# A streaming encoder step on one core: the bias table written DRAM to DRAM, and 512-column products for v and the FFN's second product

## The chip, the cores and the metric

The kernel runs on one core of a Trainium2 chip. Time is device time in microseconds (us) of one execution, lower is better. The core has TensorE (PE in the profile, with PEld for its weight loads), VectorE (DVE), ScalarE (ACT), GpSimd (POOL) and SyncE (SP). The engines run their own instruction streams in order and meet at semaphores. SP and ACT also issue DMA transfers (SPq, ACTq in the profile); the transfers themselves run on 16 DMA engines.

## What is computed

One layer of a streaming encoder for 640 tokens: 512 of a prompt and 8 samples of 16 each, with the same weights. The reference, cut to what the change touches:

```python
def rel_bias_lookup(table, rel):
    idx = jnp.clip(rel, -A_MAX_REL, A_MAX_REL) + A_MAX_REL      # 257 distances for each of 8 heads
    return jnp.transpose(table[idx], (2, 0, 1)).astype(jnp.float32)
...
    h = rmsnorm(x, lw['norm_mix'])
    a_qkv, b_qkv, b_beta, b_dec, b_gate, c_z, c_xbc, c_dt, gates = split_cols(h @ lw['w_in'], IN_SPLITS)
    aq, ak, av = [t.reshape(bsz, L, A_HEADS, A_HEAD_DIM) for t in jnp.split(a_qkv, 3, axis=-1)]
    ya = band_attn_prompt(aq, ak, av, lw['a_rel_bias'])         # s = q k * scale + bias; softmax; p v
...
    x = x + m @ lw['w_out']
    x = x + memory_attn(rmsnorm(x, lw['norm_x']), mem_k, mem_v, lw['wx_q'], lw['wx_o'])
    hf = rmsnorm(x, lw['norm_ffn'])
    u, gf = jnp.split(hf @ lw['w_up'], 2, axis=-1)
    gf, f_conv_new = causal_dwconv(gf, f_conv, lw['f_conv_w'], lw['f_conv_b'])
    x = x + (u * jax.nn.silu(gf)) @ lw['w_down']
```

The layer has three branches (chunk attention, a gated delta rule, a state-space scan), a merge, cross attention, an FFN of width 2816, and a final norm. All data are float32.

## The kernel before

Each large matrix product is made of three products in a reduced type, fp32r: both factors are split into a high part (`wh`, `hh`, `xTh`) and a low part (`wl`, `hl`, `xTl`), and high by high, low by high and high by low are accumulated in PSUM. ACT makes the high part of a weight piece (`split_w`, a copy), DVE or POOL the low part (a subtraction). A weight piece is loaded by SP into one of two `raw` buffers; the parts go to pool `wp`, six buffers for each, or to a pool of general buffers where `loose` is set. A raw buffer is free again when POOL has made the last low part from it.

There are two forms of product. `fmj` has the weight as stationary operand and streams the 640 tokens in two pieces of 320 columns. `tmj` has a tile of 128 tokens as stationary operand and streams 256 columns of weight: this is used for v (`attn_v`, PSUM name `tm`), for the output projections (`add_proj`, name `ap`) and for the FFN's second product (`add_proj` and `last_proj`, name `dn`). `add_proj` takes the 1024 output columns in four quarters; in a quarter the five token tiles go by pairs, and DVE adds each result to `x`. In the FFN the inner width comes in blocks of 8, 8 and 6 pieces of 128. `last_proj` does the last block and the final norm: after the first 512 columns ACT sums squares (`sumsq`), POOL multiplies `x` by the gain, and then the other 512 columns go pair by pair, each pair followed by its norm on DVE (`inv_rms`) and its store.

The bias table: `rel_table` loads 8 rows of 257 to 8 partitions, pads them to 384 columns on DVE, and ACT issues one store (`relt<-rel`) that writes every row 128 times to DRAM. `prompt_bias` and `attn_sample` read diagonals from it (`rel_ap`), so that each partition has its row shifted by one.

The order around the change is set in `run`: v's weights (columns 1024 to 1535 of `w_in`) are loaded and split between the norms of the token tiles; then v; then `attn_dense` for four head pairs (PSUM name `aps`, q and then k, each with one raw load; the copy out of PSUM is `aqk` on ACT, and k is transposed on PE as `t5a`); `decays` (name `dps`) is between the first and the second pair. Most of the further program is emitted by generators that are pumped beside each other, and a scheduler sets the final order of each engine.

Of the kernel before, what the change touches and what calls it, by code (L numbers as in the profile page):

```python
# [23 lines left out]
NFF = 22  # L24
EPS = 1e-6
NEG = -3.0e38
FA, FS, FB, FC, FP, FX = 0.3, 0.85, 0.95, 1.8, 1.2, 0.5
NGA, NGB, NGC = 5, 3, 5
FN, FR = 3, 1.8
FBS, FCP, FCS = 1.4, 0.9, 1.5  # L30
NWS = 1
LS, LC, LX = 3, 3, 3
SEQ = (0, 1, 2, 4, 3)
LQ = 1
SKA = 1
MAGIC = float(0x5F3759DF)

# [6 lines left out]
class Enc:  # L44
# [41 lines left out]
    def add(self, name, gen, after=()):  # L86
        self.units.append((name, gen, set(after)))
# [116 lines left out]
    def load2(self, out, in_):  # L204

# [216 lines left out]
    def rel_table(self):  # L422


        self.relt = self.dr.tile([P, 8, 384], F32, name="relt")
        t = self.U("rel", shape=(8, 384))
        self.load(t[:, 127:384], self.I["a_rel_rev"])
        self.nc.vector.tensor_copy(t[:, 0:127], t[:, 127:128].broadcast_to([8, 127]))
        self.store(self.relt.rearrange("q h c -> h q c"), t.unsqueeze(1).broadcast_to([8, P, 384]))

    def rel_ap(self, h, nq, c0, n):

        return bass.AP(tensor=self.relt.tensor, offset=self.relt.offset + h * 384 + 127 + c0,
                       ap=[[8 * 384 - 1, nq], [1, n]])
# [945 lines left out]
    def attn_sample(self):  # L1380
        nc, I = self.nc, self.I
        V4, qbd, ksm = self.V[4], self.qbd, self.ksm
        bc = self.U("bsc", shape=(P, 512))
        b16 = self.SM("b16", [P, 16])
        for hh in range(8):
            self.load(bc[16 * hh:16 * hh + 16, 384:], self.rel_ap(hh, 16, 0, P))
            self.load(b16[16 * hh:16 * hh + 16, :], self.rel_ap(hh, 16, P, 16))
        nc.gpsimd.tensor_copy(bc[:, 0:384], bc[:, 384:385].broadcast_to([P, 384]))

        bn = [self.U("bsn", shape=(P, 4, P)) for _ in range(2)]  # L1390
        for b in range(8):
# [82 lines left out]
            yield from self.weave(*([scores(b + 1)] if b < 7 else []), out(b), lead=LS if b < 7 else 0)  # L1474


    def add_proj(self, w, X, x, k0=0, nk=NK, nm="ap", tiles=range(NT), t0=0, engs=None, cols=range(4), last=None,
                 late=False):

        for c in cols:  # L1480
            def cb(pair, ps):
                for j, t in enumerate(pair):
                    xv = x[t][c // 2][:, (c % 2) * 256:(c % 2) * 256 + 256]
                    self.tt(xv, xv, ps[:, j, :256], ALU.add)
            wk = self.weights(w, c * 256, 256, k0, nk, engs)
            yield from self.tmj(lambda: wk, X, cb, tiles=tiles, nm=nm, t0=t0, late=late and c == cols[0])
# [200 lines left out]
    def ffn(self, x, X):  # L1687
        I, O = self.I, self.O
        wu, wd = I["w_up"][0], I["w_down"][0]
        lt = None  # L1690
        for f0, n in ((0, 8), (8, 8), (16, 6)):
            H = []
            for f in range(f0, f0 + n):
# [3 lines left out]
                s = []  # L1697
# [17 lines left out]
                yield from self.fmj(lambda: self.weights(wu, FF + f * P, P, 0, NK), X, gate, nm="fps", split=first)  # L1715
                yield from self.fmj(lambda: self.weights(wu, f * P, P, 0, NK), X, up, nm="ups", split=first)
            if f0 + n < NFF:
                yield from self.add_proj(wd, H, x, k0=f0, nk=n, nm="dn", late=True)
            else:
                yield from self.last_proj(wd, H, x, f0, n)  # L1720

    def last_proj(self, w, H, x, k0, nk):

        nc, O = self.nc, self.O
        g = self.grow(self.I["norm_final"])
        ss = self.SM("fss", [P, 3, NT])
        yield from self.add_proj(w, H, x, k0=k0, nk=nk, nm="dn", cols=(0, 1), late=True)
        for t in range(NT):
            self.sumsq(x[t][0], ss[:, 0, t:t + 1])
            self.tt(x[t][0], x[t][0], g[0], ALU.mult, nc.gpsimd)  # L1730
        wks = [self.weights(w, c * 256, 256, k0, nk, loose=c == 3) for c in (2, 3)]
        for pair in ((0, 1), (2, 3), (4,)):
            for c in range(2):
                def cb(pair, ps):
                    for j, t in enumerate(pair):
                        xv = x[t][1][:, c * 256:(c + 1) * 256]
                        self.tt(xv, xv, ps[:, j, :256], ALU.add)
                        self.sumsq(xv, ss[:, 1 + c, t:t + 1])
                yield from self.tmj(lambda: wks[c], H, cb, tiles=pair, nm="dn")
            r = self.inv_rms(ss[:, :, pair[0]:pair[-1] + 1])  # L1740
            for i, t in enumerate(pair):
                dst = O["y_prompt"][0, t * P:(t + 1) * P] if t < 4 else O["y_sample"].rearrange("b s d -> (b s) d")
                self.stt(x[t][1], x[t][1], r[:, i:i + 1], g[1], ALU.mult, ALU.mult)
                self.act(x[t][0], x[t][0], scale=r[:, i:i + 1])
                for j in range(2):
                    self.load(dst[:, j * 512:(j + 1) * 512], x[t][j])


    def run(self):
        I = self.I  # L1750
        all_ = lambda gen: [None for _ in gen]
# [195 lines left out]
```

## Time and the profile before

| | before |
|---|---|
| time, median of 3 runs | 1810.25 us (1808.98 to 1810.54) |
| time of the profiled execution | 1809.45 us |
| its span | 1807.7 us, 34056 instructions |
| PE busy | 1691.8 us, 94% of the span |
| PEld, DVE, ACT, POOL busy | 88%, 48%, 36%, 34% |
| mean DMA rate | 101 GB/s, 182.41 MB |

The span is what the trace covers; the profiled execution's time has 1.75 us more around it. A busy PE is the union of its matmuls' spans, which overlap, so that the spacing between their starts tells more than the length of one.

### The profile page before, as it was taken

To read this page: it belongs to the slowest core of one execution; us is meant where nothing else is said; L and a number is where in the kernel's file an instruction comes from. 1 tells how busy PE (TensorE), PEld (TensorE's weight loads), DVE (VectorE), ACT (ScalarE), POOL (GpSimd) and SP (SyncE) were. 2 spreads that over 40 slices of the span, in tenths; PEclk is the share of its full clock that TensorE was granted. 3 is DMA by queue.
4 is the path that set the end of the run, shared out by engine and by line. 5 is a ranking of instruction groups with operands and counts; after the bars stand their busy time and mean duration, and the time that the engine had idled before them with its cause. 6 is when DMAs were issued, how large, how long until landed. Compare 5 with 4: busy or idle time off the path is not lost.

```text
span 1807.7 us, 34056 instructions
## 1 busy us (share of the span) xinstructions
PE 1691.8 (94%) x13705; PEld 1585.8 (88%) x13705; DVE 862.5 (48%) x1778; ACT 652.3 (36%) x1611; POOL 613.3 (34%) x644
## 2 busy tenths in 40 slices
PE   6689999999999998999999889999989999999997
PEld 6577778888988888999999889987789999999997
DVE  5025764246777684665444463243574413431443
ACT  4024444422433432343442245332433313331333
POOL 4043322222333353453433235211144334433433
PEclk9889999999999999999999999999999999999999
DMA  5442127422321344235223335246332222212222
GB/s 157 65 113 56 50 84 257 160 67 61 79 80 52 96 123 117 74 110 147 67 74 92 137 120 160 64 170 223 116 106 73 81 71 73 81 60 77 87 78 77
DMA packets 239309, 182.41 MB, mean 101 GB/s; under 512 B 13314, under 2 KB 211983, under 8 KB 239151
## 3 DMA queue, kind: packets, MB, share of 16 engines
q1 hardware_dynamic: 216192, 164.69, 30.1%
q10 hardware_dynamic: 22958, 15.54, 3.3%
q8 instruction: 108, 1.77, 0.4%
q14 instruction: 51, 0.41, 0.1%
HBM read 162.04 MB, written 16.58 MB: 99 GB/s over the span
## 4 chain that ended last, share of the span: by engine, by line
PE 69%; DVE 10%; DMA 3%; ACT 3%; issue 2%; POOL 1%; ACTq 0%; POOLq 0%; SPq 0%; DVEq 0%
PE ups L210 9%; PE fps L210 8%; PE gps L210 8%; PE dn L210 8%; PE pps L210 6%; PE ap L210 5%; PE tm L210 4%; PE qps L210 3%; PE cps L210 2%; DVE xc L221 2%; PE bps L210 2%; PE pl L210 1%; DVE t L218 1%; PE py L210 1%; DMA raw<-in_wx_v_dram 1%
## 5 line engine op out<-in xcount | busy, mean ns | idle before, releaser
L218 POOL TENSOR_TENSOR wl<-raw,wh 128x512 fp32r<-128x512 f32 x376 | 496.5, 1329 | 973.9 <-ACT wh L224 750.5
L224 ACT ACTIVATE wh<-raw 128x512 fp32r<-128x512 f32 x400 | 248.3, 629 | 601.2 <-PE dn L210 94.6
L210 PE MATMUL dn<-wh,hh 128*128 128x256 f32 x440 | 125.1, 284 | 0.4
L210 PE MATMUL dn<-wl,hh 128*128 128x256 f32 x440 | 124.7, 283 | 0.5 <-POOL wl L218 0.5
L210 PE MATMUL dn<-wh,hl 128*128 128x256 f32 x440 | 124.5, 283 | 0.0
L221 DVE SCALAR_TENSOR_TENSOR xc<-xp,vec,xc 128x664 f32<-128x664 f32 (+1 forms) x116 | 117.3, 1011 | 3.2
L210 PE MATMUL gps<-xTh,wh 128*128 128x320 f32 x448 | 117.0, 339 | 0.0
L210 PE MATMUL gps<-xTh,wl 128*128 128x320 f32 x448 | 106.4, 316 | 0.0
L210 PE MATMUL gps<-xTl,wh 128*128 128x320 f32 x448 | 105.3, 314 | 0.0
L541 DVE TENSOR_SCALAR xc<-xp,vec 128x656 f32<-128x656 f32 (+1 forms) x34 | 32.3, 950 | 131.8 <-ACT xp L224 131.8
L210 PEld LDWEIGHTS dn<-wh,hh 128*128 128x128 f32 x440 | 84.4, 192 | 1.3 <-DVE x L218 1.0
L210 PEld LDWEIGHTS dn<-wl,hh 128*128 128x128 f32 x440 | 84.4, 192 | 0.9 <-POOL wl L218 0.9
L210 PEld LDWEIGHTS dn<-wh,hl 128*128 128x128 f32 x440 | 84.4, 192 | 0.0
L210 PEld LDWEIGHTS gps<-xTh,wh 128*128 128x128 f32 x448 | 73.8, 192 | 11.4 <-issue 10.6
L210 PE MATMUL ups<-fTh,wl 128*128 128x320 f32 x352 | 82.0, 310 | 0.0
L210 PE MATMUL fps<-fTh,wh 128*128 128x320 f32 x352 | 82.0, 310 | 0.0
L210 PE MATMUL ups<-fTl,wh 128*128 128x320 f32 x352 | 82.0, 310 | 0.0
L210 PE MATMUL ups<-fTh,wh 128*128 128x320 f32 x352 | 81.7, 310 | 0.0
L210 PE MATMUL fps<-fTh,wl 128*128 128x320 f32 x352 | 81.5, 309 | 0.0
L210 PE MATMUL fps<-fTl,wh 128*128 128x320 f32 x352 | 81.5, 309 | 0.0
L218 DVE TENSOR_TENSOR x<-x,dn 128x256 f32<-128x256 f32 x60 | 23.0, 418 | 118.5 <-PE dn L210 118.5
L210 PEld LDWEIGHTS gps<-xTh,wl 128*128 128x128 f32 x448 | 76.0, 190 | 0.9 <-issue 0.8
(517 smaller groups left out, 4564.0 us busy)
## 6 DMA issues: line engine op xcount, KB each, us to landing
raw<-in_w_in_dram SPq DMA_DIRECT2D x72, 512.0 KB
raw<-in_w_up_dram SPq DMA_DIRECT2D x44, 512.0 KB
raw<-in_w_down_dram SPq DMA_DIRECT2D x20, 512.0 KB
ck<-in_cache_attn_k_dram SPq DMA_DIRECT2D x32, 256.0 KB
cv<-in_cache_attn_v_dram SPq DMA_DIRECT2D x32, 256.0 KB
xck<-in_cache_mem_k_dram SPq DMA_DIRECT2D x32, 256.0 KB
xcv<-in_cache_mem_v_dram SPq DMA_DIRECT2D x32, 256.0 KB
raw<-in_wx_o_dram SPq DMA_DIRECT2D x14, 512.0 KB
```

The costliest lines, as they stand in the source:

```text
L210: self.nc.tensor.matmul(out, lhsT=lhsT, rhs=rhs, start=start, stop=stop)
L218: return (eng or self.nc.vector).tensor_tensor(out, a, b, op=op)
L221: self.nc.vector.scalar_tensor_tensor(out, a, s, b, op0=op0, op1=op1)
L224: self.nc.scalar.activation(out, in_, f, **kw)
L541: nc.vector.tensor_scalar(acc[:, :n], xp[:, :n], taps[0], bias, op0=ALU.mult, op1=ALU.add)
```

## The change

`rel_table` no longer goes through SBUF: one DMA from DRAM to DRAM, on SP's queue, writes the 8 by 257 table 128 times, 8224 bytes at a time and without padding, and a second small one loads the outermost value of each head to all partitions (`far`). The pad is made where it is used: after the load of a diagonal, DVE overwrites the part left of the diagonal by `copy_predicated` with a mask, and POOL fills the far columns from `far` and not from the loaded tile. The sample part gets four small DVE instructions more. `wmj` is new: 512 columns, the inner dimension as outer loop, and all five token tiles accumulated at once in five PSUM banks. `add_proj` uses it where the columns come in halves, which is the FFN's second product; the two other output projections keep quarters. `attn_v` and the second half of `last_proj` use 512 columns with one tile after another. In `last_proj` DVE and POOL share the low parts of the last weights.

```diff
+QUARTERS = ((0, 256), (256, 256), (512, 256), (768, 256))
...
+    def wmj(self, w, c0, X, cb, k0=0, nk=NK, tiles=range(NT), nm="tm", t0=0, engs=None):
+        tiles = list(tiles)
+        acc = []
+        for i in range(0, len(tiles) - 1, 2):
+            ps = self.PD(nm)
+            acc += [(tiles[i], ps[:, 0]), (tiles[i + 1], ps[:, 1])]
+        if len(tiles) % 2:
+            acc.append((tiles[-1], self.PP(nm)))
+        for k in range(nk):
+            if k % 2 == 0:
+                wk = self.weights(w, c0, 512, k0 + k, min(2, nk - k), engs)
+            wh, wl = wk[k % 2]
+            xh, xl = X[k]
+            for t, ps in acc:
+                s = slice((t - t0) * P, (t - t0 + 1) * P)
+                for p, (a, b) in enumerate(((xh, wh), (xl, wh), (xh, wl))):
+                    self.mm(ps, a[:, s], b, start=(k == 0 and p == 0), stop=(k == nk - 1 and p == 2))
+            yield 0.69 * len(acc)
+        self.tick()
+        for t, ps in acc:
+            cb(t, ps)
...
     def rel_table(self):
-        self.relt = self.dr.tile([P, 8, 384], F32, name="relt")
-        t = self.U("rel", shape=(8, 384))
-        self.load(t[:, 127:384], self.I["a_rel_rev"])
-        self.nc.vector.tensor_copy(t[:, 0:127], t[:, 127:128].broadcast_to([8, 127]))
-        self.store(self.relt.rearrange("q h c -> h q c"), t.unsqueeze(1).broadcast_to([8, P, 384]))
+        rev = self.I["a_rel_rev"]
+        self.relt = self.dr.tile([P, 8, A_REL], F32, name="relt")
+        self.load(self.relt.rearrange("q h c -> q (h c)"), rev.rearrange("h c -> (h c)").partition_broadcast(P))
+        self.far = self.C("far", [P, 8])
+        self.load(self.far, rev[:, 0].partition_broadcast(P))
...
@@ prompt_bias
-            nc.gpsimd.tensor_copy(b[:, 0:256], b[:, 256:257].broadcast_to([P, 256]))
+            far = self.far[:, 2 * p + h:2 * p + h + 1]
+            nc.gpsimd.tensor_copy(b[:, 0:256], far.broadcast_to([P, 256]))
+            nc.vector.copy_predicated(b[:, 256:384], self.ms.bitcast(I32), far.broadcast_to([P, P]))
             nc.vector.memset(b[0:64, 448:512], NEG)
...
@@ attn_v
-            for c in range(2):
...
-                yield from self.tmj(lambda: wks[c], X, cb, tiles=pair)
+            ps = self.PD("tm")
+            for j, t in enumerate(pair):
+                for k, (wh, wl) in enumerate(wks):
...
+                        self.mm(ps[:, j], a[:, t * P:(t + 1) * P], b, start=(k == 0 and p == 0),
+                                stop=(k == NK - 1 and p == 2))
...
@@ ffn, last_proj
-                yield from self.add_proj(wd, H, x, k0=f0, nk=n, nm="dn", late=True)
+                yield from self.add_proj(wd, H, x, k0=f0, nk=n, nm="dn")
...
-        wks = [self.weights(w, c * 256, 256, k0, nk, loose=c == 3) for c in (2, 3)]
+        wk = [a for k in range(0, nk, 2) for a in self.weights(w, 512, 512, k0 + k, 2, (nc.vector, nc.gpsimd), loose=k >= 4)]
```

Outside the replaced parts the order of the engines is nearly the same before and after: on PE some thirty rows move by a few places, all of them between v and the sample attention.

The first place is SP's queue at the start, behind the loads of `x`. `raw_258` and `raw_268` are the second half of v's weights, the next two raws those of the first head pair. Before:

```order
L227 DMA x_105<-in_x_sample_dram 128x512
L227 DMA x_107<-in_x_sample_dram 128x512
L227 DMA raw_258<-in_w_in_dram 128x4x256
L227 DMA raw_268<-in_w_in_dram 128x4x256
L227 DMA raw_618<-in_w_in_dram 128x8x128
L227 DMA raw_681<-in_w_in_dram 128x8x128
```

And after:

```order
L252 DMA x_105<-in_x_sample_dram 128x512
L252 DMA x_107<-in_x_sample_dram 128x512
L252 DMA relt<-in_a_rel_rev_dram 128x2056
L252 DMA far<-in_a_rel_rev_dram 128x8x1
L252 DMA raw_258<-in_w_in_dram 128x2x512
L252 DMA raw_268<-in_w_in_dram 128x2x512
```

The table and `far` now stand ahead of the last two weight loads of v.

The second place is ACT from the end of v to the copy of the first pair's k (`aqk_739` before, `aqk_610` after), for which PE's transposes `t5a` wait. Before:

```order
L224 ACTIVATE wh_687<-raw_681 128x512
L230 DMA relt<-rel_608 8x128x384
L224 ACTIVATE V_345<-tm_580 128x256
L224 ACTIVATE aqk_676<-aps_617 128x640
L230 DMA out_dram<-V_345 128x512
L224 ACTIVATE wh_852<-raw_850 128x512
L224 ACTIVATE wh_856<-raw_850 128x512
L224 ACTIVATE wh_954<-raw_952 128x512
L224 ACTIVATE wh_958<-raw_952 128x512
L224 ACTIVATE aqk_739<-aps_680 128x640
```

And after:

```order
L249 ACTIVATE V_345<-tm_452 128x512
L255 DMA out_dram<-V_345 128x512
L249 ACTIVATE wh_725<-raw_723 128x512
L249 ACTIVATE wh_729<-raw_723 128x512
L249 ACTIVATE aqk_547<-aps_488 128x640
L249 ACTIVATE wh_827<-raw_825 128x512
L249 ACTIVATE wh_831<-raw_825 128x512
L249 ACTIVATE wh_889<-raw_887 128x512
L249 ACTIVATE wh_893<-raw_887 128x512
L249 ACTIVATE aqk_610<-aps_551 128x640
```

The store of the table is gone from ACT, and the splits of three raw loads, not of two, stand ahead of the copy for which PE waits.

The third place is the last half of the last FFN block, on POOL and on PE. On POOL `x_` by `grow_` are the gain products of the first 512 columns, `wl_` low parts of the last weights. Before:

```order
L218 TENSOR_TENSOR x_11346<-x_11346,grow_19516 128x512
L218 TENSOR_TENSOR x_11350<-x_11350,grow_19516 128x512
L218 TENSOR_TENSOR wl_19783<-raw_19780,wh_19782 128x512
L218 TENSOR_TENSOR wl_19787<-raw_19780,wh_19786 128x512
L218 TENSOR_TENSOR wl_19793<-raw_19790,wh_19792 128x512
```

And after:

```order
L243 TENSOR_TENSOR x_11228<-x_11228,grow_18890 128x512
L243 TENSOR_TENSOR x_11232<-x_11232,grow_18890 128x512
L243 TENSOR_TENSOR x_11236<-x_11236,grow_18890 128x512
L243 TENSOR_TENSOR wl_19065<-raw_19058,wh_19064 128x512
```

On PE after the change, twelve products into `dn_19068` (the second half's first tile) precede these:

```order
L235 MATMUL dn_19137<-wh_19040,hh_18165 128x512
L235 MATMUL dn_19068<-wh_19060,hh_18738 128x512
L235 MATMUL dn_19068<-wh_19060,hl_18739 128x512
L235 MATMUL dn_19137<-wh_19040,hl_18166 128x512
L235 MATMUL dn_19068<-wl_19061,hh_18738 128x512
L235 MATMUL dn_19068<-wh_19064,hh_18886 128x512
L235 MATMUL dn_19068<-wh_19064,hl_18887 128x512
L235 MATMUL dn_19068<-wl_19065,hh_18886 128x512
```

The low part that POOL makes behind all five gain products, `wl_19065`, is now taken as PE's twentieth product of the half; before, the low parts behind the gain products belonged to the last quarter.

## Rows read from the trace of the kernel before

**Rows 1.** The page, busy time of each engine (share of the span) and instructions.

```profile
PE 1691.8 (94%) x13705; PEld 1585.8 (88%) x13705; DVE 862.5 (48%) x1778; ACT 652.3 (36%) x1611; POOL 613.3 (34%) x644
```

**Rows 2.** Timeline of PE, 57 to 100 us: start, length, instruction [idle before <-releaser].

```profile
57.07 0.46 PE L210 MATMUL aps<-xTh,wh 128*128 128x320 f32 x2
...
71.24 1.26 PE L210 MATMUL dps<-xTh,rawd 128*32 128x320 f32 x10
99.00 1.12 PE L215 MATMUL t5a<-ident,aqk 128*128 128x128 f32 x4 [26.49 <-ACT aqk L224]
```

**Rows 3.** Timeline of ACT, 55 to 100 us.

```profile
55.87 0.54 ACTq L230 DMA_DIRECT2D relt<-rel  x1
...
90.07 1.15 ACT L224 ACTIVATE wh<-raw 128x512 fp32r<-128x512 f32 x2 [25.06 <-DMA raw<-in_w_in_dram]
97.21 1.15 ACT L224 ACTIVATE wh<-raw 128x512 fp32r<-128x512 f32 x2 [5.99 <-DMA raw<-in_w_in_dram]
98.26 0.68 ACT L224 ACTIVATE aqk<-aps 128x640 f32<-128x640 f32 x1
```

**Rows 4.** Timelines of SP and of POOL, 55 to 100 us.

```profile
58.34 35.32 SPq L227 DMA_DIRECT2D raw<-in_w_in_dram  x2
...
55.76 2.55 POOL L218 TENSOR_TENSOR wl<-raw,wh 128x512 fp32r<-128x512 f32 x2 [21.79 <-ACT wh L224]
90.78 2.49 POOL L218 TENSOR_TENSOR wl<-raw,wh 128x512 fp32r<-128x512 f32 x2 [32.47 <-ACT wh L224]
```

**Rows 5.** DMA queues, 55 to 100 us: packets, MB, share of 16 engines (q10 ACT's, q1 SP's).

```profile
q10 hardware_dynamic: 1176, 1.84, 33.5%
q1 hardware_dynamic: 2080, 1.05, 8.5%
```

**Rows 6.** Windows: length, busy time of five engines, granted clock, DMA share, GB/s.

```profile
10.00:12.00 2.00, 0.65 (x4) 0.25 (x2) 0.01 (x1) 1.65 (x4) 1.95 (x2) 1.00 1.05 387
34.00:36.00 2.00, 0.44 (x3) 0.47 (x4) 1.86 (x7) 0.00 (x0) 0.00 (x0) 0.91 0.72 51
36.00:38.00 2.00, 2.00 (x11) 2.00 (x10) 2.00 (x4) 1.27 (x4) 0.00 (x0) 0.50 0.28 23
80.00:85.00 5.00, 0.00 (x0) 0.00 (x0) 0.00 (x0) 0.00 (x0) 0.00 (x0) 0.50 0.50 65
```

**Rows 7.** Timelines of ACT, POOL and DVE, 16 to 24 us.

```profile
17.74 1.15 ACT L224 ACTIVATE wh<-raw 128x512 fp32r<-128x512 f32 x2 [2.33 <-DMA raw<-in_w_in_dram]
...
18.44 6.49 POOL L218 TENSOR_TENSOR wl<-raw,wh 128x512 fp32r<-128x512 f32 x4 [3.42 <-ACT wh L224]
...
18.00 5.79 DVE L221 SCALAR_TENSOR_TENSOR xn<-x,y,grow 128x512 f32<-128x512 f32 x4
```

**Rows 8.** Timeline of DVE, 105 to 215 us.

```profile
143.43 0.29 DVE L1336 CUSTOM_DVE_ANT_0 ae<-asp,bias 128x128 f32<-128x128 f32 x1
```

**Rows 9.** Timeline of PE, in cross attention and in the last FFN block.

```profile
1194.91 1.32 PE L210 MATMUL xpo<-xpT,mv 128*128 128x512 f32 x5
1196.07 0.28 PE L210 MATMUL xsp<-mKT,xqh 128*128 128x256 f32 x1
...
1790.13 0.28 PE L210 MATMUL dn<-wl,hh 128*128 128x256 f32 x1
...
1793.01 0.28 PE L210 MATMUL dn<-wl,hh 128*128 128x256 f32 x1
```

**Rows 10.** Timelines of ACT, POOL, PE and DVE, from 1774 us to the end.

```profile
1774.07 0.63 ACT L224 ACTIVATE junk<-x 128x512 f32<-128x512 f32 x1 [2.98 <-DVE x L218]
...
1774.87 3.81 POOL L218 TENSOR_TENSOR x<-x,grow 128x512 f32<-128x512 f32 x3 [1.77 <-ACT junk L224]
...
1798.05 0.28 PE L210 MATMUL dn<-wl,hh 128*128 128x256 f32 x1
...
1798.29 1.41 DVE L221 SCALAR_TENSOR_TENSOR x<-x,y,grow 128x512 f32<-128x512 f32 x2
1799.62 0.41 DVE L218 TENSOR_TENSOR x<-x,dn 128x256 f32<-128x256 f32 x1
1800.66 0.16 DVE L469 TENSOR_REDUCE v<-fss 128x1 f32<-128x3 f32 x1 [0.64 <-ACT junk L224]
```

More of the change, by code (lines that the diff above doesn't have):

```diff
@@ L26 @@
 NEG = -3.0e38
+A_REL = 257
 FA, FS, FB, FC, FP, FX = 0.3, 0.85, 0.95, 1.8, 1.2, 0.5
@@ L30 @@
 FBS, FCP, FCS = 1.4, 0.9, 1.5
-NWS = 1
 LS, LC, LX = 3, 3, 3
@@ L1254, in attn_v @@
         for pair in ((0, 1), (2, 3), (4,)):
-            for c in range(2):
-                def cb(pair, ps):
-                    for j, t in enumerate(pair):
-                        self.act(V[t][:, c * 256:(c + 1) * 256], ps[:, j, :256])
-                yield from self.tmj(lambda: wks[c], X, cb, tiles=pair)
-            for t in pair:
+            ps = self.PD("tm")
+            for j, t in enumerate(pair):
+                for k, (wh, wl) in enumerate(wks):
+                    xh, xl = X[k]
+                    for p, (a, b) in enumerate(((xh, wh), (xl, wh), (xh, wl))):
+                        self.mm(ps[:, j], a[:, t * P:(t + 1) * P], b, start=(k == 0 and p == 0),
+                                stop=(k == NK - 1 and p == 2))
+                    yield 0.69
+                self.tick()
+                self.act(V[t], ps[:, j])
                 self.store(O["attn_v_prompt"][0, 0].rearrange("s h d -> s (h d)")[t * P:(t + 1) * P] if t < 4 else
@@ L1387, in attn_sample @@
             self.load(b16[16 * hh:16 * hh + 16, :], self.rel_ap(hh, 16, P, 16))
-        nc.gpsimd.tensor_copy(bc[:, 0:384], bc[:, 384:385].broadcast_to([P, 384]))
+        fr = self.SM("far8", [P, 8])
+        self.tt(fr, self.far, self.blkc, ALU.mult)
+        f1 = self.SM("far1", [P, 1])
+        nc.vector.tensor_reduce(f1, fr, axis=AX.X, op=ALU.add)
+        low = self.SM("low", [P, 16])
+        nc.vector.tensor_reduce(low, self.ms_s.rearrange("p (a c) -> p c a", c=16), axis=AX.X, op=ALU.add)
+        nc.vector.copy_predicated(bc[:, 384:400], low.bitcast(I32), f1.broadcast_to([P, 16]))
+        nc.gpsimd.tensor_copy(bc[:, 0:384], f1.broadcast_to([P, 384]))
         bn = [self.U("bsn", shape=(P, 4, P)) for _ in range(2)]
@@ L1474, in attn_sample, with add_proj, add @@
             yield from self.weave(*([scores(b + 1)] if b < 7 else []), out(b), lead=LS if b < 7 else 0)
-    def add_proj(self, w, X, x, k0=0, nk=NK, nm="ap", tiles=range(NT), t0=0, engs=None, cols=range(4), last=None,
-                 late=False):
-        for c in cols:
+    def add_proj(self, w, X, x, k0=0, nk=NK, nm="ap", tiles=range(NT), t0=0, engs=None, cols=((0, 512), (512, 512)),
+                 last=None):
+        for c0, n in cols:
+            def add(t, ps):
+                xv = x[t][c0 // 512][:, c0 % 512:c0 % 512 + n]
+                self.tt(xv, xv, ps, ALU.add)
             def cb(pair, ps):
                 for j, t in enumerate(pair):
[L1483 to L1486, printed above, removed]
+                    add(t, ps[:, j, :n])
+            if n == 512:
+                yield from self.wmj(w, c0, X, add, k0, nk, tiles, nm, t0, engs)
+                continue
+            wk = self.weights(w, c0, n, k0, nk, engs)
+            yield from self.tmj(lambda: wk, X, cb, tiles=tiles, nm=nm, t0=t0)
             if last:
@@ L1725, in last_proj @@
         g = self.grow(self.I["norm_final"])
-        ss = self.SM("fss", [P, 3, NT])
-        yield from self.add_proj(w, H, x, k0=k0, nk=nk, nm="dn", cols=(0, 1), late=True)
+        ss = self.SM("fss", [P, 2, NT])
+        yield from self.add_proj(w, H, x, k0=k0, nk=nk, nm="dn", cols=((0, 512),))
         for t in range(NT):
@@ L1730, in last_proj @@
             self.tt(x[t][0], x[t][0], g[0], ALU.mult, nc.gpsimd)
-        wks = [self.weights(w, c * 256, 256, k0, nk, loose=c == 3) for c in (2, 3)]
+        wk = [a for k in range(0, nk, 2) for a in self.weights(w, 512, 512, k0 + k, 2, (nc.vector, nc.gpsimd), loose=k >= 4)]
         for pair in ((0, 1), (2, 3), (4,)):
[L1733 to L1739, printed above, removed]
+            ps = self.PD("dn")
+            for j, t in enumerate(pair):
+                for k, (wh, wl) in enumerate(wk):
+                    hh, hl = H[k]
+                    for p, (a, b) in enumerate(((hh, wh), (hl, wh), (hh, wl))):
+                        self.mm(ps[:, j], a[:, t * P:(t + 1) * P], b, start=(k == 0 and p == 0),
+                                stop=(k == nk - 1 and p == 2))
+                    yield 0.69
+                self.tt(x[t][1], x[t][1], ps[:, j], ALU.add)
+                self.sumsq(x[t][1], ss[:, 1, t:t + 1])
             r = self.inv_rms(ss[:, :, pair[0]:pair[-1] + 1])
@@ L1754, in run @@
         w = I["w_in"][0]
-        raws = [self.raw(w, 1024, 256, 4 * a, 4) for a in range(2)]
+        raws = [self.raw(w, 1024, 512, 2 * a, 2) for a in range(2)]
         x0 += [self.load_x(t) for t in range(1, NT)]
@@ L1870, in run @@
         both = (self.nc.gpsimd, self.nc.vector)
-        self.add("WP", self.add_proj(I["wx_o"][0], OX, x, tiles=range(4), cols=range(4 - NWS)), after=("XP",))
+        self.add("WP", self.add_proj(I["wx_o"][0], OX, x, tiles=range(4), cols=QUARTERS[:3]), after=("XP",))
         cur = None
@@ L1887, in run @@
         self.need("WP")
-        self.add("WL", self.add_proj(I["wx_o"][0], OX, x, tiles=range(4), engs=both, cols=range(4 - NWS, 4), last=OS))
-        self.add("WS", self.add_proj(I["wx_o"][0], OS, x, tiles=(4,), t0=4, engs=both, cols=range(4 - NWS)))
+        self.add("WL", self.add_proj(I["wx_o"][0], OX, x, tiles=range(4), engs=both, cols=QUARTERS[3:], last=OS))
+        self.add("WS", self.add_proj(I["wx_o"][0], OS, x, tiles=(4,), t0=4, engs=both, cols=QUARTERS[:3]))
         self.need("WL")
```

10 lines of the change are left out of this document (5 added, 5 removed).

## The prediction

> **What bounds the kernel now.** I read the busy shares first: PE is busy for 94% of the span, no other engine for half of it [rows 1]. So a change counts where PE waits, or where it changes how fast PE streams. The timeline of PE shows one long wait: after v ends at 57.07 PE runs the first head pair's products and part of `dps`, is out of work at 72.5, and starts `t5a` at 99.00 after 26.49 us of idling [rows 2]. Its releaser is ACT's copy `aqk`, but ACT itself was held: the copy stands behind the splits of two raw loads, and ACT waited 25.06 us and then 5.99 us for these [rows 3]. The first was issued at 58.34 and reached ACT at 90.07; the second shares its buffer, could be issued only when POOL was done with the first (90.78 + 2.49 = 93.27), and reached ACT 3.9 us later [rows 3, 4].
>
> Why 31.7 us for a load whose successor took 3.9? The DMA queues answer. From 55 to 100 us ACT's queue used 33.5% of 16 engines for 45 us, 241 us of engine time, for 1.84 MB, nearly all of it the table's store issued at 55.87; SP's queue used 8.5% for twice as many packets [rows 3, 5]. In the middle of the stall the DMA share stands at 0.50 with 65 GB/s [rows 6]: 8 of 16 engines, one for each of the store's 8 rows, and 241 / 8 = 30 us is how long the store ran. The load's pieces on these 8 engines came in beside its slow packets (205 ns each: 241 us by 1176), and the load was complete when the store was.
>
> **The change, part by part.** I measure from the end of v, 57.07.
>
> First the stall. With the store gone, a load takes the 3.9 us of the second one, and a buffer is free 3.20 us after landing (90.07 to 93.27). But three loads now precede `aqk`, all through one buffer, the other being held by `dps`. First load: issued at +1.27, lands at +5.2, buffer free at +8.4. Second: +12.3 and +15.5. Third: +19.4, its two copies 1.05 us (97.21 to 98.26), `aqk` and the hand-over 0.74: `t5a` at +21.2. Before it stood at +41.9: **-20.7 us**. PE is out of its own work at +15.4, so a stall of 5.8 us stays. Bounds: -26.5 if PE never waits; -14.5 if each load takes 6 us.
>
> Second, where the table goes. It is written at about 11 us, in SP's queue ahead of the last two weight loads of v. The next work behind these is ACT's split of `raw_258` at 17.74, which already waited 2.33 us for its load [rows 7], and PE waits for the low parts that follow. The DMA engines are then full: 1.05 of share and 387 GB/s [rows 6]. The trace has no DRAM-to-DRAM transfer. Lower bound: 1.05 MB at 387 GB/s, 2.7 us. Upper: the store's engine time, 241 us for 1.84 MB, scaled to 1.05 MB and spread over 16 engines since the outermost dimension is 128: 8.6 us. I take 5.4, twice the lower, since each byte is read from and written to DRAM; the long rows and full spread are nearer the loads than the store. `far` is 1024 pieces of 4 bytes; the three `rawd` loads of 1024 short pieces each fill 0.72 x 2 + 0.28 x 2 = 2.0 us of the DMA in 34 to 38 us [rows 6], so 0.7. Something comes back: POOL's four low parts took 6.49 us beside DVE's four `xn` (5.79 us) [rows 7], but 1.25 us each when alone [rows 4]. `xn` needs no delayed load and will be done before: -1.5. Together **+4.5 us** (1.9 to 7.8).
>
> Third, the products. Five 512-column products of the same type in cross attention start 1.16 / 5 = 232 ns apart; 256-column ones in the FFN 2.88 / 24 = 120 ns apart [rows 9]. Two narrow ones cost 240, a wide one 232: 8 ns for each of 660 wide products of the FFN (22 pieces x 3 x 5 tiles x 2 halves): **-5.3 us**. In v 120 replace 240, but the first ones run at POOL's pace; I count 74, those that stand behind the last norm's transposes: **-0.6**. [...] The five banks held at once are no wait: DVE's adds of the first tiles come while the last piece still runs on the others, and the six weight buffers are freed piece by piece.
>
> [...]
>
> Fourth, the last half. With T the end of the first half on PE, five adds, five sums of squares (0.63 us each [rows 10]) and five gain products (3.81 / 3 = 1.27 us [rows 10]) follow each other. The first tile's add can end at T - 1.9 and its sum of squares at T - 1.1, so POOL is done with five products at about T + 5.3, and with `wl_19065` at T + 6.5. PE takes it as its twentieth product, at 19 x 0.232 = T + 4.4: a new stall of **+2.1 us** (0 to 4). Nothing hides it: PE is what ends last there.
>
> Fifth, the end. PE's last product starts at 1798.05, but the last add waits behind DVE's 1.41 us of the previous pair and the norm chain starts at 1800.66 [rows 10], 2.3 us after PE's end at 1798.33. After, the add of 512 columns (0.7 for 0.41) comes first and that 1.41 us between it and the norm: 0.15 + 0.7 + 0.4 + 1.4 = 2.7. **+0.4** (0 to 1).
>
> Sixth, the bias. Eight `copy_predicated` of 128 x 128, not in the trace; an instruction of that shape on DVE takes 0.29 us [rows 8], and 1.0 would be the most. That is 2.3 us of DVE time, up to 8, in a stage where PE now and then waits for DVE: **+0.8** (0 to 4). The wait for the loaded diagonal is not new on DVE, as the `memset` behind it had it. The small sample instructions fall where DVE is idle.
>
> Sum: -20.7 + 4.5 - 5.3 - 0.6 + 2.1 + 0.4 + 0.8 = -18.8. Against the profiled execution's 1809.45 (0.8 below the median of 1810.25) that is 1790.7; I say **1791 us**.
>
> **The rivals.** (a) *The table is slow in its new place*: at the store's engine time the start costs 7.8, and with more contention 11; what speaks for it is that the store was slow while other transfers weren't, and I don't see which side of it. 1794 to 1798, say 1796. (b) *The stall keeps more*: three loads in line, beside v's stores, at 6 us each: -14.5, 1797. [...] (d), the other side: *the table blocks the queue*. If the copy is confined to few engines, v's weights behind it wait: on one engine at 387 / 16 = 24 GB/s it takes 44 us, the start costs about 42, and the time is 1828. It decides from a start of 23 us on, when it eats all the rest. Against it: 128 rows outermost, where the store had 8. (e) *The store isn't the cause* of the late load: then the stall stays, a third load adds 7 us, and the time is about 1819. Against it speak the share of exactly one half and the load's end with the store's.
>
> **How the numbers follow.** Forecast 0.48, (a) 0.17, (b) 0.12, (c) 0.10, (d) 0.06, (e) 0.04, and 0.03 for small losses that together cancel the gain. The range leaves out (d), (e) and the ends of the bounds: 1781 (the stall gone whole, -5.8, with some of (c)) to 1801 ((a) or (b) with no gain of the wide products). Changes within 0.2%, 3.6 us, can't be told from none. Faster 0.88, same 0.03, slower 0.09.
>
> **What would show it.** In the profile after: `t5a` some 21 us after v's end with 5 to 6 us of idle before it; a table transfer on SP's queue that ends before 25 us, with a DMA share near 1 and not 0.5; ACT's split of `raw_258` at 22 to 24 us; `dn` at 128x512 every 232 ns; a wait of PE for POOL's `wl` of about 2 us some 17 us before PE's end. I am wrong if the split of `raw_258` comes after 30 us, or if raw loads between 58 and 80 us still take more than 8 us.

## The result, and the profile after

| | before | changed |
|---|---|---|
| time, median (runs) | 1809.62 us (4) | 1787.72 us (1786.85 to 1791.73, 4) |
| ratio | | 0.9885, 95% interval 0.9867 to 0.9903 |
| profiled execution, its span | 1809.45, 1807.7 | 1787.08, 1785.4 |

The changed kernel takes 1.15% less, 3.3 us less than the 1791 of the forecast. The sum was nearly right because terms that were off cancelled, so it is taken apart here by places that both programs have. PE's idle time names most of them. The timeline of PE in the changed kernel, at the start, at the first k's transposes, behind the decays, and in the last half:

```profile
21.42 0.80 PE L235 MATMUL tm<-wh,xTh 128*128 128x512 f32 x1 [4.36 <-ACT wh L249]
...
37.36 0.63 PE L240 MATMUL nps<-ident,xn 128*128 128x128 f32 x4 [2.55 <-DVE xn L246]
...
57.16 0.45 PE L235 MATMUL aps<-xTh,wh 128*128 128x320 f32 x2
...
78.60 1.12 PE L240 MATMUL t5a<-ident,aqk 128*128 128x128 f32 x4 [6.00 <-ACT aqk L249]
...
94.49 0.66 PE L240 MATMUL t5a<-ident,dsb 128*128 128x128 f32 x4 [1.08 <-ACT dsb L249]
...
1757.39 1.22 PE L235 MATMUL dn<-wl,hh 128*128 128x512 f32 x2 [2.62 <-POOL wl L243]
```

Against [rows 2] the 26.49 us ahead of `t5a` are 6.00, v's end stands at 57.16 for 57.07, and a wait of 2.62 us is new. What ACT does ahead of `aqk`, beside [rows 3]:

```profile
62.57 1.15 ACT L249 ACTIVATE wh<-raw 128x512 fp32r<-128x512 f32 x2 [4.61 <-DMA raw<-in_w_in_dram]
...
69.64 1.15 ACT L249 ACTIVATE wh<-raw 128x512 fp32r<-128x512 f32 x2 [4.54 <-DMA raw<-in_w_in_dram]
76.81 1.15 ACT L249 ACTIVATE wh<-raw 128x512 fp32r<-128x512 f32 x2 [6.01 <-DMA raw<-in_w_in_dram]
77.86 0.68 ACT L249 ACTIVATE aqk<-aps 128x640 f32<-128x640 f32 x1
```

Three loads, one after the other, 7.1 us apart; none takes 30. The table's own transfer is issued on SP at 11.51, and the split of `raw_258` comes 3.0 us later than in [rows 7]: at 20.74, ahead of the 22 to 24 that I gave. Timelines of SP and ACT at the start:

```profile
11.51 0.61 SPq L252 DMA_DIRECT2D relt<-in_a_rel_rev_dram  x1
...
20.74 1.15 ACT L249 ACTIVATE wh<-raw 128x512 fp32r<-128x512 f32 x2 [5.34 <-DMA raw<-in_w_in_dram]
```

Windows over the table's transfer and the two weight loads behind it, with the columns of [rows 6]:

```profile
12.00:14.00 2.00, 2.00 (x4) 1.36 (x5) 1.36 (x2) 2.00 (x6) 2.00 (x3) 1.00 1.08 400
14.00:16.00 2.00, 2.00 (x6) 1.52 (x6) 0.51 (x4) 1.39 (x6) 1.17 (x1) 1.00 1.02 389
16.00:18.00 2.00, 1.06 (x5) 0.54 (x3) 1.65 (x12) 0.00 (x0) 0.00 (x0) 1.00 0.83 247
18.00:20.00 2.00, 0.00 (x0) 0.00 (x0) 2.00 (x4) 0.00 (x0) 0.00 (x0) 0.87 1.01 358
```

The share is 0.83 to 1.08 (247 to 400 GB/s), with no stretch at one half as in [rows 6]. In the last half, timelines of PE and POOL:

```profile
1761.12 0.39 PE L235 MATMUL dn<-wl,hh 128*128 128x512 f32 x1
...
1767.24 0.39 PE L235 MATMUL dn<-wl,hh 128*128 128x512 f32 x1
...
1749.39 6.73 POOL L243 TENSOR_TENSOR x<-x,grow 128x512 f32<-128x512 f32 x5 [4.45 <-ACT junk L249]
1756.08 1.26 POOL L243 TENSOR_TENSOR wl<-raw,wh 128x512 fp32r<-128x512 f32 x1
```

Between the first two rows lie 27 steps in 6.12 us: 226.7 ns for a wide product, against 240 for two narrow ones [rows 9]. `wl`, for which PE waits, stands behind all five gain products. Windows there (the granted clock is the number ahead of the last two; in windows of 1 us over both kernels it stands between 0.50 and 1.00, and wide products start 0.43 us apart where it is 0.50, in 1758.40 to 1760.12, for 0.227 at 1.00):

```profile
1754.00:1757.40 3.40, 0.78 (x4) 0.30 (x3) 0.00 (x0) 0.00 (x0) 3.34 (x3) 0.92 0.00 0
1757.40:1760.40 3.00, 3.00 (x7) 2.40 (x8) 0.69 (x1) 0.72 (x2) 0.00 (x0) 0.52 0.00 0
1760.40:1764.00 3.60, 3.60 (x17) 2.98 (x16) 0.00 (x0) 0.00 (x0) 0.00 (x0) 1.00 0.00 0
```

The clock is 0.52 for the 3 us behind the wait, and then 1.00 again.

From such places, the ledger (differences of PE's starts and ends in the two profiled executions):

| stretch | forecast | measured |
|---|---|---|
| start, to v's end | +4.5 - 0.6 | +0.1 |
| v's end to `t5a` (41.93 to 21.44) | -20.7 | -20.5 |
| `t5a` to 109 us (28.87 to 30.58) | +0.8 for the bias, here and in the next row | +1.7 |
| 109 us to the FFN's first `dn` | in the row above | +1.5 |
| first `dn` to the last `ups` (313.66 to 306.56), 480 wide products | -3.8 | -7.1 |
| the last `ups` to PE's end (45.10 to 46.59), 180 wide products and a wait | -1.4 + 2.1 | +1.5 |
| PE's end to the end | +0.4 | +0.5 |

### The profile page after: what moved, and what is told of

Its sections match the earlier page's. It is cut to its first block, busy times and chain, and to the rows that moved or that the text cites. A ratio compares the mean times of both kernels' runs of the same rounds, so it can differ in the third digit from the quotient of the medians.

```text
span 1785.4 us, 32450 instructions
## 1 busy us (share of the span) xinstructions
PE 1683.1 (94%) x12925; PEld 1542.6 (86%) x12925; DVE 860.4 (48%) x1762; ACT 650.5 (36%) x1596; POOL 607.4 (34%) x641
## 4 chain that ended last, share of the span: by engine, by line
PE 69%; DVE 10%; DMA 4%; ACT 3%; issue 2%; POOL 1%; ACTq 0%; SPq 0%; POOLq 0%; DVEq 0%
PE ups L235 9%; PE fps L235 9%; PE gps L235 8%; PE dn L235 8%; PE pps L235 6%; PE ap L235 5%; PE tm L235 4%; PE qps L235 3%; PE cps L235 2%; DVE xc L246 2%; PE bps L235 2%; PE pl L235 1%; DVE t L243 1%; PE py L235 1%; PE xkt L240 1%
## 5 line engine op out<-in xcount | busy, mean ns | idle before, releaser
L243 POOL TENSOR_TENSOR wl<-raw,wh 128x512 fp32r<-128x512 f32 x373 | 490.8, 1321 | 961.3 <-ACT wh L249 791.3
L235 PE MATMUL dn<-wl,hh 128*128 128x512 f32 x220 | 86.4, 394 | 2.9 <-POOL wl L243 2.6
L235 PE MATMUL dn<-wh,hh 128*128 128x512 f32 x220 | 86.3, 393 | 0.1
L235 PE MATMUL dn<-wh,hl 128*128 128x512 f32 x220 | 85.8, 391 | 0.0
L235 PEld LDWEIGHTS gps<-xTl,wh 128*128 128x128 f32 x448 | 76.1, 191 | 0.7 <-issue 0.6
L235 PE MATMUL tm<-wh,xTh 128*128 128x256 f32 (+1 forms) x200 | 65.5, 327 | 8.6 <-ACT wh L249 4.4
L243 DVE TENSOR_TENSOR x<-x,dn 128x512 f32<-128x512 f32 x30 | 19.3, 683 | 108.1 <-PE dn L235 107.7
L235 PE MATMUL tm<-wh,xTl 128*128 128x256 f32 (+1 forms) x200 | 63.6, 318 | 0.2 <-DVE xTl L243 0.2
```

The costliest lines, as they stand in the source:

```text
L235: self.nc.tensor.matmul(out, lhsT=lhsT, rhs=rhs, start=start, stop=stop)
L243: return (eng or self.nc.vector).tensor_tensor(out, a, b, op=op)
```

## The experiments

Ratios are to the kernel before, run on the same chip; times in the text are of the profiled executions. In six profiles of kernels whose programs are the same up to v, v's end lies between 57.16 and 59.73 us, so positions are compared as distances.

| run | ratio (95%) | run | ratio (95%) |
|---|---|---|---|
| table alone | 0.9896 (0.9876 to 0.9916) | changed kernel again | 0.9866 (0.9843 to 0.9888) |
| wide products alone | 0.9935 (0.9919 to 0.9951) | last low parts on DVE | 0.9850 (0.9835 to 0.9865) |
| table later on SP | 0.9859 (0.9842 to 0.9876) | own buffers for the decays | 0.9842 (0.9821 to 0.9863) |
| store from 16 rows | 0.9940 (0.9921 to 0.9959) | wide output projection | 0.9900 (0.9883 to 0.9917) |
| control, 8 rows | 1.0011 (0.9992 to 1.0030) | both remedies | 0.9812 (0.9785 to 0.9839) |

**The table alone.** The kernel before with the change's `rel_table`, `rel_ap`, `prompt_bias` and `attn_sample`.

```diff
-        self.store(self.relt.rearrange("q h c -> h q c"), t.unsqueeze(1).broadcast_to([8, P, 384]))
+        self.load(self.relt.rearrange("q h c -> q (h c)"), rev.rearrange("h c -> (h c)").partition_broadcast(P))
```

> The kernel before with the new table alone (the DRAM-to-DRAM write, far, the mask), all products at 256 columns. Theory (the store held the load for which ACT waits; its end frees some 20 us): t5a about 21 us after v's end as in the changed kernel, the start 3 us later and no gain from wide products: -20.5 + 3 + 1.7 (what the changed kernel lost again between 80 and 109 us) = about 1793.5. Rival (the stall went because the wide v reordered ACT's splits and copies, not because of the store): t5a stays 35 us or more behind v's end, and the time is 1805 or more.

Median 1795.97, -18.8 us by the ratio. The timeline of PE:

```profile
81.99 1.12 PE L216 MATMUL t5a<-ident,aqk 128*128 128x128 f32 x4 [6.39 <-ACT aqk L225]
```

v ended at 60.16, so `t5a` stands 21.8 us behind it, as in the changed kernel; no wide product was needed for that. The rival is out. From the first `dn` to the last `ups` (313.64 us), and on to PE's end (45.13), nothing moved.

**The wide products alone.** The changed kernel with those four functions from the kernel before.

```diff
-        self.load(self.relt.rearrange("q h c -> q (h c)"), rev.rearrange("h c -> (h c)").partition_broadcast(P))
+        self.store(self.relt.rearrange("q h c -> h q c"), t.unsqueeze(1).broadcast_to([8, P, 384]))
```

> The changed kernel with the old table (8 rows through SBUF, the store on ACT). Rival (parts add): the stall of 26 us stays and only the products gain, about -5.1 in the FFN and -1.6 in v: 1803. Theory that looks at the order: here k's copy aqk stands on ACT right behind the store and ahead of the splits that wait for the late load, so t5a comes without a long wait; the load behind the store still lands some 30 us after the store's issue, PE has 12 to 14 us more of work by then, and waits some 12 us at k of the second head pair instead of 26: about 1788 to 1791.

Median 1801.52, -11.8 us. Timelines of ACT and PE:

```profile
72.29 0.70 ACT L249 ACTIVATE aqk<-aps 128x640 f32<-128x640 f32 x1 [6.33 <-PE aps L235]
97.77 1.15 ACT L249 ACTIVATE wh<-raw 128x512 fp32r<-128x512 f32 x2 [24.78 <-DMA raw<-in_w_in_dram]
105.60 1.15 ACT L249 ACTIVATE wh<-raw 128x512 fp32r<-128x512 f32 x2 [4.75 <-DMA raw<-in_w_in_dram]
...
107.39 1.11 PE L240 MATMUL t5a<-ident,dsb 128*128 128x128 f32 x4 [21.73 <-ACT dsb L249]
```

The order was as I said: the first `t5a` came at 73.04 without a long wait. The price was not. PE stood 21.73 us at the next `t5a`, which waits for the decays' copy `dsb`, and that stands on ACT behind the splits of two late loads; I had counted one. The number is near the rival's 1803, by another way: the stall is not kept in its place, it moves with the order, and the store's duration sets what is left. The FFN's 480 products gave 7.1 us here too (306.53). The two parts alone add up to 30.6 us, and the whole change is worth 20.8: part of the gain here is the shorter stall (21.73 us for 26.49), which the new table takes away by itself.

**The store from 16 rows, and its control with 8.** The kernel before, with the table head by head in DRAM; the control has 8 partitions as source in the same layout.

```diff
-        self.relt = self.dr.tile([P, 8, 384], F32, name="relt")
-        t = self.U("rel", shape=(8, 384))
+        self.relt = self.dr.tile([8, P, 384], F32, name="relt")
+        t = self.U("rel", shape=(16, 384))
...
-        self.store(self.relt.rearrange("q h c -> h q c"), t.unsqueeze(1).broadcast_to([8, P, 384]))
+        self.store(self.relt.rearrange("h (d q) c -> (h d) q c", d=2), t.unsqueeze(1).broadcast_to([16, 64, 384]))
```

> The kernel before with the store of the table from 16 partitions (each head twice, 64 copies each) into a table laid out head by head; the same 1.57 MB, the same place on ACT's queue. Theory (8 rows outermost put it on 8 of 16 engines): the DMA share goes to about 1 while it runs, it takes 15 us and not 30, the load behind it lands at 73 to 76 and not at 90 us, t5a at 82 to 84, and the time is 1792 to 1795. Rival (the store is slow for another reason, its packets of 1536 bytes out of few partitions): share 0.5 or less, 26 us of stall, 1809.

> The control of the run with 16 source rows: the same head-by-head layout of the table in DRAM, but 8 partitions as source. Theory (the number of source rows sets the number of engines): share 0.5 and 50 GB/s while the store runs, 30 us, t5a at 99 to 100, the time of the kernel before within 3 us. Rival (the layout in DRAM, one contiguous run, spread the store): share 0.88 and 17 us as with 16 rows, about 0.994 of the kernel before.

Median 1801.85 with 16 rows (-10.9 us) and 1812.78 with 8. A window while the store runs and the timeline of PE, with 16 rows:

```profile
66.00:70.00 4.00, 4.00 (x29) 4.00 (x28) 0.44 (x2) 0.07 (x1) 0.00 (x0) 1.00 0.87 97
```

```profile
88.06 1.11 PE L215 MATMUL t5a<-ident,aqk 128*128 128x128 f32 x4 [14.50 <-ACT aqk L224]
```

The same two views with 8 rows:

```profile
82.00:86.00 4.00, 0.00 (x0) 0.00 (x0) 0.00 (x0) 0.00 (x0) 0.00 (x0) 0.50 0.49 64
```

```profile
100.96 1.11 PE L215 MATMUL t5a<-ident,aqk 128*128 128x128 f32 x4 [27.19 <-ACT aqk L224]
```

The same bytes with the same packets: share 0.87 for 0.49, 17.0 us of store for 32.9 by the packets in the trace, and 12.7 us less of stall. The layout in DRAM alone changes nothing (with 8 rows in it the share is 0.49 and the time 1812.78): what differs between these two runs is the number of source rows. The load behind the store was split at 79.12, later than the 73 to 76 that I gave, `t5a` came at 88.06 and not at 82 to 84, and the time missed 1792 to 1795. The trace says why: with 16 rows none of the load's 1024 packets ran between 58 and 73 us, while the store had the engines at a share of 0.85. In the kernel before, 512 of them ran by 62 us, none from 62 to 72, and the others came in beside the store's until 89.4: half of the load came in within 4 us of its issue at 58.34, and half only from 72 us on. So what held the load is shown. Why a store from few rows is slow is not: it moved 48 GB/s from 8 rows and 97 from 16, some 6 for each row, and no run changes the engines without the rows.

**The table later on SP.** The changed kernel with `rel_table` behind the loads of the first head pair.

```diff
-        self.rel_table()
         self.need("A0")
         with self.tc.issue_after(self.last_raw.ins):
+            self.rel_table()
             self.loads()
```

> The changed kernel with the table and far issued behind the loads of the first head pair and not ahead of v's last two weight loads. Theory (the table's transfer costs the start 3 us): the split of raw_258 back at 17.7 us and not 20.7, v's end at about 54 and not 57.2, everything behind it as much earlier: 1784.5. Rival (the start is bound by POOL's low parts and DVE, the table was hidden): v's end stays within 0.5 us, 1787. Rival (the table now delays the loads of the first head pair's k, the decays and the third raw): t5a not earlier, 1787 or more.

Median 1788.47; the interval overlaps those of the changed kernel. Timelines of ACT and PE of this run, and a window:

```profile
17.68 1.15 ACT L249 ACTIVATE wh<-raw 128x512 fp32r<-128x512 f32 x2 [2.11 <-DMA raw<-in_w_in_dram]
...
37.08 1.09 PE L240 MATMUL nps<-ident,xn 128*128 128x128 f32 x4 [2.96 <-DVE xn L246]
```

```profile
37.00:41.00 4.00, 3.92 (x17) 3.58 (x18) 3.22 (x5) 1.92 (x4) 0.00 (x0) 0.50 0.50 40
```

PE's timeline and the window in the changed kernel's second run:

```profile
37.74 1.08 PE L240 MATMUL nps<-ident,xn 128*128 128x128 f32 x4 [2.62 <-DVE xn L246]
```

```profile
37.00:41.00 4.00, 3.26 (x15) 2.93 (x16) 3.41 (x6) 1.79 (x4) 0.00 (x0) 0.57 0.35 30
```

POOL's low parts, with the later table and then in the changed kernel's second run:

```profile
18.39 6.72 POOL L243 TENSOR_TENSOR wl<-raw,wh 128x512 fp32r<-128x512 f32 x4 [3.06 <-ACT wh L249]
```

```profile
21.53 4.98 POOL L243 TENSOR_TENSOR wl<-raw,wh 128x512 fp32r<-128x512 f32 x4 [6.37 <-ACT wh L249]
```

The split is back at 17.68, and v's end is at 59.46 (58.72 in the second run). My theory falls, and the first rival is right in kind. Of the 3 us, 1.7 come back at once: started earlier, POOL's four low parts run beside DVE's `xn` and take 6.72 us for 4.98, and PE waits for them. The rest shrinks at 37 us, where PE waits for the norms `xn` of the last token tiles. The run with the later table reached that wait 1.0 us earlier, waited longer (2.96 for 2.62), and had no better clock behind it.

**The last low parts on DVE.**

```diff
-        wk = [... self.weights(w, 512, 512, k0 + k, 2, (nc.vector, nc.gpsimd), loose=k >= 4)]
+        wk = [... self.weights(w, 512, 512, k0 + k, 2, (nc.vector, nc.vector if k >= 4 else nc.gpsimd), loose=k >= 4)]
```

> The changed kernel with both low parts of the last two weight pieces on DVE, so that none stands behind POOL's five gain products. Theory (PE waits 2.62 us for POOL's last low part, and then runs some 2 us longer because the clock fell to 0.52 for the 3 us behind the wait): both go, -4 to -4.6, that is 0.9975 of the changed kernel. Rival (only the wait goes, the clock falls anyway, or PE then waits for DVE, which also holds the five adds): -2.6 or less.

Median 1784.35 against 1786.82 on the same chip, and intervals that overlap; the stretch from the last `ups` to PE's end is 3.2 us shorter (46.78 to 43.55). Timelines of DVE and PE, and a window:

```profile
1753.28 2.99 DVE L243 TENSOR_TENSOR wl<-raw,wh 128x512 fp32r<-128x512 f32 x2 [1.35 <-ACT wh L249]
...
1756.32 0.73 PE L235 MATMUL dn<-wl,hh 128*128 128x512 f32 x2 [0.73 <-DVE wl L243]
```

```profile
1757.00:1759.00 2.00, 2.00 (x10) 1.43 (x9) 0.55 (x1) 0.72 (x2) 0.41 (x1) 1.00 0.00 0
```

The clock stays at 1.00, as the theory had it; 0.73 us of wait stay, since DVE's two low parts took 1.5 us each beside POOL's gain products (0.69 us each when POOL rests, in the half before). The stretch lies between theory and rival. The medians differ by 2.5 us, which is the rival's number; of its reasons, the wait for DVE came true and the fall of the clock did not.

**Own buffers for the decays.**

```diff
-        raw = self.wp.tile([P, 8, 32], F32, name="rawd", tag="raw", bufs=2)
+        raw = [self.Q("rawd").rearrange("p (k c) -> p k c", c=32) for _ in range(2)]
...
-            self.load(raw[:, :, c:c + n], wv[:, :, c0:c0 + n])
+            for a in range(2):
+                self.load(raw[a][:, :, c:c + n], wv[:, 4 * a:4 * a + 4, c0:c0 + n])
```

> The changed kernel with the weights of the decays in two small buffers of their own, so that both raw buffers are free for the three loads ahead of the first k's copy. Theory (the 6.0 us that are left of the stall are three loads through one buffer, one after the other): the first of the three is loaded before v ends, the third split waits only for a weight buffer at about 71.5, t5a at 73 and not at 78.6, and the clock does not fall: -5.6 for the wait and up to -2.5 for the clock, together -6 to -8. Rival (ACT's order holds the copy: the splits ahead of it wait for weight buffers that PE frees late, whatever the loads do): t5a at 77 or later, -1.5 at most.

Median 1782.72, 4.1 us less than the changed kernel beside it (the intervals overlap). Timelines of ACT and PE, and a window:

```profile
73.10 0.63 ACT L249 ACTIVATE wh<-raw 128x512 fp32r<-128x512 f32 x1 [2.90 <-PE aps L235]
...
74.42 0.66 PE L240 MATMUL t5a<-ident,aqk 128*128 128x128 f32 x4
```

```profile
75.00:79.00 4.00, 4.00 (x58) 1.88 (x56) 0.16 (x1) 1.17 (x4) 0.08 (x1) 1.00 0.70 179
```

No wait is left ahead of `t5a`, the split ahead of the copy waits for a weight buffer and no load, and the clock is 1.00. At the decays' end the run is 8.0 us ahead of the changed kernel (79.27 to 87.23), as the theory said; at the first `dn` 2.8 us of that are left in this execution, which was the slowest of its four (1779.5 to 1786.6). From the last `ups` to PE's end another 1.4 us go (48.17 for 46.78): behind the same wait of 2.62 us the clock stayed at 0.50 for 6 us, not for 3. Where the others go I can't say.

**A wide output projection.** The changed kernel with halves there too.

```diff
-        all_(self.add_proj(I["w_out"][0], M, x, cols=QUARTERS))
+        all_(self.add_proj(I["w_out"][0], M, x))
```

> The changed kernel with 512-column products in the output projection of the merge too (240 wide products in place of 480). Theory (13.3 ns for each wide product, 240 ns for two narrow ones against 226.7 ns): -3.2. Rival (its five adds come together at the end of a half, the norm that follows starts later, and PE has too little other work there): 0 or a loss of 1 to 3.

Median 1793.20 against 1786.82: 6.4 us slower, more than the rival had (the intervals overlap at their ends, but each of its runs is slower than every run of the changed kernel beside it). Timeline of PE and a window in this run, then the window in the changed kernel beside it:

```profile
994.03 1.11 PE L240 MATMUL nps<-ident,xn 128*128 128x128 f32 x4 [4.17 <-DVE xn L246]
997.34 1.11 PE L240 MATMUL nps<-ident,xn 128*128 128x128 f32 x4 [2.20 <-DVE xn L246]
1003.70 1.97 PE L240 MATMUL nps<-ident,xn 128*128 128x128 f32 x8 [5.25 <-DVE xn L246]
```

```profile
995.00:1005.00 10.00, 2.55 (x11) 2.01 (x11) 5.67 (x21) 2.68 (x9) 0.00 (x0) 0.50 0.16 59
```

```profile
995.00:1005.00 10.00, 10.00 (x86) 9.99 (x85) 5.62 (x16) 4.44 (x12) 1.56 (x2) 1.00 0.08 28
```

The rival's norm behind the projection is not the place: the transposes `nps` of the memory's norm stand on PE between the two halves with nothing among them, PE waits 11.6 us for them (1.94 and 4.23 in the changed kernel, where they lie among products), and the clock is 0.50. Here wide products cost more than they save.

**Both remedies.** The decays' buffers, and in `last_proj` the weights emitted ahead of the sums and gain products, so that on POOL the last low parts come first.

```diff
+        wk = [a for k in range(0, nk, 2) for a in self.weights(...)]
         for t in range(NT):
             self.sumsq(x[t][0], ss[:, 0, t:t + 1])
             self.tt(x[t][0], x[t][0], g[0], ALU.mult, nc.gpsimd)
-        wk = [a for k in range(0, nk, 2) for a in self.weights(...)]
```

> The kernel with the decays' weights in their own buffers, and in the last half all low parts ahead of the gain products on POOL, DVE's ahead of its five adds (none of them then waits for the five gain products). Theory: both waits that the changed kernel has left go, t5a at 74 to 75 and no wait over 1 us in the last half with the clock at 1.00 there; -4 of the decays' buffers and -4 to -4.6 of the last half: 1778 to 1780. Rival (the adds now wait behind the low parts, and the final norms end later): no more than the decays' buffers alone, 1782 to 1784.

Median 1776.66, -34 us by the ratio, and `t5a` at 74.93 without a wait; the interval is wholly below those of the changed kernel. POOL's timeline and a window:

```profile
1743.95 6.31 POOL L243 TENSOR_TENSOR x<-x,grow 128x512 f32<-128x512 f32 x5 [3.91 <-ACT junk L249]
```

```profile
1745.00:1750.00 5.00, 5.00 (x23) 3.96 (x22) 1.36 (x3) 2.18 (x8) 5.00 (x5) 1.00 0.00 0
```

The clock is 1.00 and PE has no gap where the wait had been, though the gain products run at the same time; and from the last `ups` to PE's end it takes 42.05 us for 46.59: the wait and the slower clock behind it had cost 4.5. In three other profiles with the same wait (wide products alone, later table, own buffers) the stretch takes 47.9 to 48.2 us, with the clock at or near 0.50 for 6 us: there the two cost about 6. The adds behind DVE's low parts don't show.

## Why the prediction was right, and where its terms were not

*What bounds the kernel.* Right, and shown. The store from 8 rows, at a share of 0.50, held the load, the load held ACT, ACT held PE; the table alone gives -18.8 us, and 16 source rows halve the store (17.0 us for 32.9).

*The stall, -20.7.* Measured -20.5, by the steps given: splits at +5.4, +12.5 and +19.7 behind v's end (I had +5.2, +12.3, +19.4), 6.00 us of stall left (5.8). That these come from one buffer is shown by the decays' own buffers.

*The table in its new place, +4.5.* The step that failed. I priced 6.1 us of delay for the loads behind it (5.4 for the table, 0.7 for `far`), and the split came 3.0 later, near the lower bound of 2.7. The 1.5 that I took back was about right (1.7). But I took all that was left for PE's loss and did not ask what PE waits for next; [rows 6, 7] had DVE's work of the norms in view. At v's end 0.1 us is left in this pair of executions. That is in part luck: v ends at 57.16 to 59.73 in the six profiles with the changed start and at 57.07 to 58.33 in the three with the old one, so by their means about 1 us may be left. With the table alone, and narrow products, it ended at 60.16, in one profile.

*The products, -5.3 in the FFN.* Mis-sized: 13.3 ns a product and not 8, 14.8 over the blocks (the further 1.5 is not explained), so 660 x 14.8 = 9.8. My 232 ns came from five products of cross attention, which are 228 to 236 ns apart there; nine in ten of the FFN's are 226 or 227. Why these are closer no run shows. The chance of (c), wide products that gain more than these 8 ns, and its part in the lower end of the range rest on no run: how much more was my estimate. What the runs showed is the 9.8, 4.5 above my term; other terms had to cancel for the time to end only 3.3 us below the forecast.

*The last half, +2.1.* Right in place and kind, too small: 4.2 in the ledger (1.5 + 180 x 14.8 ns), 4.5 by the run with both remedies. The wait was 2.62 and 0.28, and the clock at 0.52 for the 3 us behind it (products up to 0.43 us apart) cost the rest. No term of mine had the clock behind a new wait, and its price is not fixed: 3 us at 0.52 in this execution, 6 at or near 0.50 in three others.

*The end, +0.4, and the bias, +0.8.* The end came out at +0.5. The bias was right in kind and too small. The eight copies took 0.23 to 1.32 us each on DVE, where I had 1.0 as the most. PE doesn't wait for the first pair's two, but for the second pair's. DVE and PE there, before:

```profile
152.53 0.34 DVE L1306 TENSOR_SCALAR ae<-ae,ers 128x384 f32<-128x384 f32 x1
...
153.31 0.66 PE L210 MATMUL apo<-apT,V 128*64 128x128 f32 x8 [0.23 <-DVE apT L1355]
```

And in the changed kernel:

```profile
133.58 0.31 DVE L1347 COPY_PREDICATED bias<-ms,far 128x128 f32<-128x128 int32 x1
...
134.08 1.39 DVE L1337 TENSOR_SCALAR ae<-ae,ers 128x384 f32<-128x384 f32 x1
...
135.93 0.66 PE L235 MATMUL apo<-apT,V 128*64 128x128 f32 x8 [1.28 <-DVE apT L1388]
```

Behind the two copies DVE's multiplication starts just after a low part on POOL (133.99 to 135.27) and takes 1.39 us for 0.34; before, it started ahead of POOL's (152.72). That POOL stretches it is read from these times and not tested. The wait of 1.28 us stands in all eight profiles with the new table, and is 0.23 or less in the four with the old one. PE's waits ahead of `apo` come to 6.7 us together in the changed kernel, for 5.2 before: this is the +1.5 behind 109 us. Of the 1.7 us lost up to 109 us, 1.08 is the wait for `dsb` and 0.4 the slower clock on the decays.

With these, -18.8 becomes -22.3 (the profiled executions differ by 22.37): -3.8 at the start, -4.5 in the products, +2.1 in the last half, +2.4 in between, +0.3 for the stall and the end.

## What to carry to other kernels

Before a slow transfer is moved, count the rows of its slowest dimension: here the same bytes took 17.0 us from 16 rows and 32.9 from 8, and the load queued beside them was split at 79.12 and not at 92.07. A delay is priced at the next wait of the bounding engine, not where it arises (3.0 us at the split of `raw_258` were 0.1 at v's end); and a new wait is priced with the clock behind it (2.62 us of wait, 4.5 with the 3 us at 0.52). A few short instructions can push a longer one behind another engine's start, and cost more than their own time (0.34 us became 1.39 behind two copies of 0.24 to 0.31, as read from the times and not tested). A wider product did not pay where something that PE must wait for stood alone between its halves: 6.4 us more, with 11.6 us of waits there.

## What the runs showed that I had not expected

The start is not the same from run to run: the changed kernel waited 2.55 us for `xn` in one run and kept its clock at 1.00 from 37 to 41 us, and waited 2.62 us in the other and had 0.57; v ended at 57.16 and at 58.72. The store is slow on each engine, not only on few engines: with 16 rows 97 GB/s at a share of 0.87, 7 GB/s for each busy engine, where loads had 387 at 1.05 [rows 6], 23 for each.
